# Split weights written at a start that moves by 16 bytes from one block of output columns to the next

## The chip, the cores and the metric

One Trainium2 chip; the program runs on one core. The metric is the device time of one execution, in microseconds (us). Of the kernel before there are three timed runs and one profiled execution.

## What is computed

Two decoder layers over 256 tokens of width 2048, in float32, and a last RMSNorm. Layer 0 mixes tokens by attention (compressed blocks, selected blocks and a sliding window, 16 heads), layer 1 by a chunkwise matrix memory (mLSTM, 8 heads); after each mixer comes a feed-forward part with a three-tap convolution and a gate:

```python
for i in range(DEPTH):                      # DEPTH = 2
    xn = rms_norm(x, norm_mix[i])
    x = x + mixer_i(xn)                     # nsa_mixer, then mlstm_mixer
    x = x + conv_glu_ffn(rms_norm(x, norm_ffn[i]), ...)
return rms_norm(x, norm_final)
...
def conv_glu_ffn(xn, w_up, conv_w, conv_b, w_down):
    u = xn @ w_up                           # 2048 x 11264
    c = conv_b + three taps of u along the tokens
    return (silu(c[..., :5632]) * c[..., 5632:]) @ w_down
```

Nearly all the work is in the products with weights: 2048 x 5168 into the attention, 2048 x 2048 out of it, 2048 x 6160 into the mLSTM, 2048 x 2048 out of it, and per feed-forward part 2048 x 11264 up and 5632 x 2048 down.

## The kernel before, in words

**Three matmuls for one product.** TensorE multiplies in float32r, a shortened float32. To keep float32's accuracy each operand is split into a high half (rounded to float32r) and a low half (what is left), and each product is made of high x high, high x low and low x high, all added up in one PSUM bank. The activations stand transposed in `xh` and `xl` (16 tiles of 128 x 256), later in `gh`/`gl` (feed-forward), `oh`/`ol` (attention) and `moh`/`mol` (mLSTM).

**The weights** come through `load_split` (L179 to L192): a DMA on SyncE's queue brings a piece of at most 128 x 1024 into `raw` (4 buffers), ScalarE copies it to `whi` (L189) and VectorE subtracts to get `wlo` (L191); both have 5 buffers (`SPB`). The matmuls of a piece then read `whi` and `wlo`.

**Two forms of product.** In the columns form (`cols_piece`, L217 to L230, called four times for one block of 256 output columns) the weights are the stationary operand, 128 x 128 at a time, and `xh` or `xl` is the moving one, 256 columns: L225 is xh by whi, L227 xl by whi, L228 xh by wlo. A block has 16 x 2 x 3 = 96 such matmuls. It serves the way up in the feed-forward parts (44 blocks per layer) and the queries and keys. In the rows form (`rows_mm`, L194 to L199) the activations are stationary and the weights move, 512, 416, 412, 304 or 256 columns at a time: L197 and L199 with whi, L198 with wlo. `project_out` (L308 to L344) uses it for the outputs of the mixers and for the way down, one piece of 1024 columns per 128 rows of the weight, each cut into two moving operands of 512; `rows_times` (L201 to L212) uses it for the values, gates and output gates.

**Order.** Matmuls of weights form one stream on TensorE; other work (attention, mLSTM heads, convolution) is put between pieces by hand, through the lists `evacs` and `side`, one step per `tick`. The weights run ahead of TensorE as far as the five buffers reach.

**Places in memory.** The tiles' starts within a partition follow from the order and sizes of the pools' tiles. Unused tiles were put in to shift them: `pad_w` (L75, 192 bytes), `pad_x` (L92, 64 bytes), `pad_m` (L685) and one in `ffn` (L856). In the layout of the program before, counted modulo 256 bytes, `xh` and `xl` start at 96, every buffer of `raw`, `whi` and `wlo` at 32, and `gh`, `gl`, `oh`, `ol`, `moh` and `mol` at 32. All slices of `whi`, `wlo` and the activations that matmuls read in blocks of 128, 256 or 512 columns begin at multiples of 512 bytes behind these starts; the second slice of a piece of 304, 412 or 416 columns does not (for 412 it begins 1648 bytes on).

**Two small buffers.** `q_out` (L502 to L508) makes `qu` and the rotated `qr` of a pair of heads, 3 buffers each; units of four heads read them at L548 (scores) and L523. `Head.sums` makes two tiles `y` per mLSTM head (L802 to L805, 4 buffers), which `Head.turn` reads at L812.

Of the kernel before, what the change touches and what calls it, by code (L numbers as in the profile page):

```python
# [12 lines left out]
F32 = mybir.dt.float32  # L13
F32R = mybir.dt.float32r
# [7 lines left out]
P = 128  # L22
D = 2048
KT = D // P
S = 256
# [5 lines left out]
DV = 256  # L31
# [2 lines left out]
EPS = 1e-6  # L34
QSCALE = float(np.float32(128 ** -0.5))
CAP = 15.0
NEG = -1e30

C_ID, C_MQ, C_MT, C_CA, C_C1, C_RP = 0, 0, 128, 256, 288, 320
# [4 lines left out]
def host_consts():  # L44
    c = np.zeros((P, C_N), np.float32)
    i = np.arange(P)
    c[:, C_ID:C_ID + P] = np.eye(P, dtype=np.float32)
    c[:, P + C_MQ:P + C_MQ + P] = np.where(i[None, :] <= i[:, None], 0.0, NEG)
    c[:, P + C_MT:P + C_MT + P] = np.where(i[:, None] <= i[None, :], 0.0, NEG)
    j = np.arange(NCMP)  # L50
    for t in range(NT):
        ok = (16 * j[None, :] + 31 <= (t * P + i)[:, None]) & (j[None, :] < NCMP - 1)
        c[:, P + C_CA + t * NCMP:P + C_CA + (t + 1) * NCMP] = np.where(ok, 0.0, NEG)
        c[:, P + C_C1 + t * NCMP:P + C_C1 + (t + 1) * NCMP] = np.where(ok, 1.0, 0.0)
# [8 lines left out]
def trunk(ctx: ExitStack, tc: tile.TileContext, x, positions, nsa_w_in, nsa_gate_b, nsa_cmp_pe,  # L63
# [8 lines left out]
    const = ctx.enter_context(tc.tile_pool(name="const", bufs=1))  # L72
    main = ctx.enter_context(tc.tile_pool(name="main", bufs=1))
    wpool = ctx.enter_context(tc.tile_pool(name="wpool", bufs=1))
    wpool.tile([P, 48], F32, name="pad_w")  # L75
    small = ctx.enter_context(tc.tile_pool(name="small", bufs=2))
    psum = ctx.enter_context(tc.tile_pool(name="psum", bufs=8, space=PSUM))

# [2 lines left out]
    def nm(s):  # L81
        uid[0] += 1
        return f"{s}_{uid[0]}"

    def bank():
        return psum.tile([P, 512], F32, name=nm("bank"), tag="bank")

    def fview(t):
        return t.bitcast(F32)

    h = main.tile([P, NT, D], F32, name="h")
    main.tile([P, 16], F32, name="pad_x")  # L92
    xh = main.tile([P, KT, S], F32R, name="xh")
    xl = main.tile([P, KT, S], F32R, name="xl")

# [42 lines left out]
    def rsqrt(y, v):  # L138
        t = small.tile([P, 1], F32, name=nm("rsq"), tag="rsq")
        ve.tensor_scalar(y.bitcast(I32), v.bitcast(I32), -0.5, float(0x5f3759df), op0=ALU.mult, op1=ALU.add)  # L140
        ve.tensor_scalar(v, v, -0.5, None, op0=ALU.mult)
        for _ in range(3):
            ve.scalar_tensor_tensor(t, y, v, y, op0=ALU.mult, op1=ALU.mult)
            ve.scalar_tensor_tensor(y, t, 1.5, y, op0=ALU.add, op1=ALU.mult)

    RAWB, SPB, PTB = 4, 5, 4
# [24 lines left out]
    def queued(engine):  # L171
        return tc.issue_after(fence[engine]) if engine in fence else nullcontext()
# [3 lines left out]
    def preload(w, k0, nk, c0, n):  # L176
        ready[w.tensor.name, w.offset, k0, c0] = load_split(w, k0, nk, c0, n)

    def load_split(w, k0, nk, c0, n):  # L179
        got = ready.pop((w.tensor.name, w.offset, k0, c0), None)  # L180
        if got is not None:
            return got
        view = lambda t: t[:, :nk * n].rearrange("p (k c) -> p k c", k=nk)
        raw = wpool.tile([P, 1024], F32, name=nm("raw"), tag="raw", bufs=RAWB)
        nc.sync.dma_start(view(raw), w[k0 * P:(k0 + nk) * P, c0:c0 + n].rearrange("(k p) c -> p k c", p=P))
        hi = wpool.tile([P, 1024], F32R, name=nm("whi"), tag="whi", bufs=SPB)
        lo = wpool.tile([P, 1024], F32R, name=nm("wlo"), tag="wlo", bufs=SPB)
        with queued("act"):
            latest["act"] = act(view(hi), view(raw), AF.Copy).ins  # L189
        with queued("ve"):  # L190
            latest["ve"] = ve.tensor_sub(view(lo), view(raw), fview(view(hi))).ins  # L191
        return view(hi), view(lo)  # L192
# [8 lines left out]
    def rows_times(w, c0, n, nk):  # L201
        accs = [bank() for _ in range(NT)]
        for k0 in range(0, KT, nk):
            m = min(nk, KT - k0)
            hi, lo = load_split(w, k0, m, c0, n)
            run_hooks()
            for i in range(m):
                kt = k0 + i
                for t in range(NT):
                    rows_mm(hi, lo, i, xh, xl, kt, t, accs[t][:, :n], 0, n, kt == 0, kt == KT - 1)  # L210
            tick()
        return accs  # L212
# [133 lines left out]
    def nsa(norm, nxt):  # L346
        with tc.tile_pool(name="nsa", bufs=1) as pool, tc.tile_pool(name="nsw", bufs=2) as wk:
            w = nsa_w_in[0]
# [54 lines left out]
            def rope(dst, src):  # L403
                shp = [32, 2, S]
                sw = wk.tile(shp, F32, name=nm("sw"), tag="sw", bufs=1)
                ve.stream_shuffle(sw, src, swap)
                ve.tensor_mul(sw, sw, sin[:, None, :].to_broadcast(shp))
                ve.tensor_mul(dst, src, cos[:, None, :].to_broadcast(shp))
                ve.tensor_add(dst, dst, sw)
# [91 lines left out]

            def q_out(pair, ps):  # L502
                qu = wk.tile([P, 2, S], F32, name=nm("qu"), tag="qu", bufs=3)
                qr = wk.tile([P, 2, S], F32, name=nm("qr"), tag="qr", bufs=3)
                ve.tensor_mul(qu, ps, rq[:, None, :].to_broadcast([P, 2, S]))
                act(qr, qu, AF.Copy)
                rope(qr[:32], qu[:32])
                q[pair] = (qu, qr)  # L508
# [158 lines left out]
            for pair in range(8):  # L667
                ps = cols_times(w, pair * 256)
                if pair == 1:
                    drain()  # L670
                    side.append(lambda: None)
                    side.extend(attention())
                evacs.append(partial(q_out, pair, ps))
            project_out(nsa_w_out[0], oh, ol, HEADS, nxt, gate_kt=12)

    def mlstm(norm, nxt):
        with tc.tile_pool(name="mls", bufs=1) as pool, tc.tile_pool(name="mlw", bufs=2) as wk:
            w = mlstm_w_in[0]
# [20 lines left out]
            def og_out(c, accs):  # L699
# [7 lines left out]
                if c == 4:  # L707
                    act(gp, gp, AF.Tanh, scale=float(np.float32(1 / CAP)))
                    ve.tensor_scalar(li, gp[:, :, :MH], CAP, None, op0=ALU.mult)

            def log_gates():
                act(u, gp[:, :, MH:], AF.Exp, scale=-CAP)
                ve.tensor_scalar(w1p, u, 1.0, None, op0=ALU.add)
                ve.scalar_tensor_tensor(u, w1p, 1.0, u, op0=ALU.subtract, op1=ALU.subtract)
                ve.reciprocal(lf, w1p)
                ve.tensor_mul(u, u, lf)
                act(lf, w1p, AF.Ln)
                ve.tensor_sub(lf, u, lf)
                ve.tensor_scalar(rq, norm.rbc, QSCALE, None, op0=ALU.mult)
# [39 lines left out]
            class Head:  # L759
# [18 lines left out]
                def sums(self):  # L778
                    hh, a = self.hh, self.a
                    n0, n1 = bank(), bank()  # L780
                    mm(n0[:, :DV + 1], a[:, :P], v1[:, 0, hh, :], start=True, stop=True)
                    mm(n1[:, :DV + 1], a[:, P:256], v1[:, 0, hh, :], start=True, stop=False)
                    mm(n1[:, :DV + 1], a[:, 256:384], v1[:, 1, hh, :], start=False, stop=True)
                    s = wk.tile([P, NT], F32, name=nm("mss"), tag="mss")
                    d = wk.tile([P, NT], F32, name=nm("mdn"), tag="mdn")
                    c = wk.tile([P, NT], F32, name=nm("mc"), tag="mc")
                    for t, n in enumerate((n0, n1)):
                        junk = wk.tile([P, DV], BF16, name=nm("mj"), tag="mj", bufs=1)
                        act(junk, n[:, :DV], AF.Square, scale=1.0 / 16, accum_out=s[:, t:t + 1])
                        ve.tensor_scalar(d[:, t:t + 1], n[:, DV:DV + 1], -1.0, ecol[:, t, hh:hh + 1],  # L790
                                         op0=ALU.mult, op1=ALU.max)
                        ve.tensor_tensor(d[:, t:t + 1], d[:, t:t + 1], n[:, DV:DV + 1], op=ALU.max)
                    ve.reciprocal(d, d)
                    ve.tensor_mul(s, s, d)
                    ve.tensor_mul(s, s, d)
                    ve.tensor_scalar(s, s, EPS, None, op0=ALU.add)
                    for t in range(NT):
                        rsqrt(c[:, t:t + 1], s[:, t:t + 1])
                    ve.tensor_mul(c, c, d)
                    self.y = []  # L800
                    for t, n in enumerate((n0, n1)):
                        y = wk.tile([P, DV], F32, name=nm("y"), tag="y", bufs=4)  # L802
                        ve.scalar_tensor_tensor(y, n[:, :DV], c[:, t:t + 1], sog[:, t, hh * DV:(hh + 1) * DV],
                                                op0=ALU.mult, op1=ALU.mult)
                        self.y.append(y)  # L805
# [191 lines left out]
```

## Time and profile before

| | |
|---|---|
| three timed runs | 2221.68 us median (2221.18 to 2223.4) |
| profiled execution, its own time | 2222.36 us |
| its span, first to last instruction | 2220.6 us |
| mean granted TensorE clock | 0.999 of full speed |
| busy: TensorE matmul / weight load | 99% / 92% of the span |
| busy: VectorE / ScalarE / GpSimd | 65% / 50% / 1% |
| DMA | 403 MB, 182 GB/s on average |

A record of a matmul is longer than the time by which the next one follows it, since matmuls overlap in TensorE's pipeline; what a matmul costs a full stream is read from the starts of two records and the number of matmuls between them. PE stands for the matmuls, PEld for the loads of the stationary operand, DVE for VectorE, ACT for ScalarE.

### The profile page before, as it was taken

Reading aid. Unit: us, or ns where it says so; the run is one execution under the profiler, and the core shown is the slowest. Engines: PE = TensorE matmul, PEld = TensorE weight load, DVE = VectorE, ACT = ScalarE, POOL = GpSimd, SP = SyncE. Lnnn points to the kernel's source line nnn. Section 1 sums busy time; section 2 is a strip of 40 time slices with the busy share of each in tenths; the row PEclk is TensorE's granted clock in tenths of the full one; section 3 lists DMA queues with packets and bytes.
Section 4 is the critical chain, followed back from the end, with each engine's and each line's share of the span. In section 5 each row is a group of like instructions: output and inputs, shape, how many; then the busy total and the mean of one; then the engine's idle time right before and its main releaser. Section 6 shows DMA issues by size and latency. Waiting matters only on the chain.

```text
span 2220.6 us, 37284 instructions
## 1 busy us (share of the span) xinstructions
PE 2203.8 (99%) x15072; PEld 2042.1 (92%) x15072; DVE 1444.2 (65%) x2191; ACT 1113.4 (50%) x1565; POOL 19.1 (1%) x56
## 2 busy tenths in 40 slices
PE   9999999999999999999999999999999999999998
PEld 8899789999999899998899988899999899998987
DVE  6488757676656666665645665667666566675755
ACT  6366655554445454454654444555545454454544
POOL 2000000000000000000000000000000000000000
PEclk9999999999999999999999999999999999999999
DMA  8653355666666666666567655566666666666664
GB/s 242 204 166 106 112 162 180 189 183 190 188 191 189 191 187 186 192 187 191 165 187 200 171 171 167 169 197 191 188 191 184 193 185 189 190 187 192 184 195 133
DMA packets 298317, 403.33 MB, mean 182 GB/s; under 512 B 12904, under 2 KB 256840, under 8 KB 298016
## 3 DMA queue, kind: packets, MB, share of 16 engines
q1 hardware_dynamic: 297264, 399.03, 59.6%
q8 instruction: 118, 1.93, 0.4%
q0 software_dynamic: 688, 1.83, 0.3%
q14 instruction: 55, 0.45, 0.1%
q10 hardware_dynamic: 192, 0.08, 0.0%
HBM read 398.80 MB, written 2.10 MB: 181 GB/s over the span
## 4 chain that ended last, share of the span: by engine, by line
PE 97%; DMA 1%; ACT 1%; DVE 1%; issue 0%; SPq 0%; ACTq 0%
PE bank L225 18%; PE bank L228 18%; PE bank L227 18%; PE bank L197 13%; PE bank L199 13%; PE bank L198 13%; DMA raw<-in_nsa_w_in_dram 1%; PE bank L548 1%; PE bank L259 1%; PE bank L579 0%; DMA h<-in_x_dram 0%; ACT whi L189 0%; ACT pr L552 0%; PE bank L523 0%; DVE wlo L191 0%; PE bank L597 0%
## 5 line engine op out<-in xcount | busy, mean ns | idle before, releaser
L191 DVE TENSOR_TENSOR wlo<-raw,whi 128x1024 fp32r<-128x1024 f32 (+3 forms) x755 | 912.6, 1210 | 609.8 <-ACT whi L189 607.4
L189 ACT ACTIVATE whi<-raw 128x1024 fp32r<-128x1024 f32 (+3 forms) x755 | 790.4, 1048 | 955.3 <-PE bank L227 483.5
L225 PE MATMUL bank<-xh,whi 128*128 128x256 f32 x3456 | 970.4, 281 | 3.2 <-ACT whi L189 2.6
L228 PE MATMUL bank<-xh,wlo 128*128 128x256 f32 x3456 | 965.8, 280 | 1.5 <-DVE wlo L191 1.5
L227 PE MATMUL bank<-xl,whi 128*128 128x256 f32 x3456 | 965.4, 279 | 0.1
L225 PEld LDWEIGHTS bank<-xh,whi 128*128 128x128 f32 x3456 | 649.1, 188 | 7.7 <-ACT whi L189 3.4
L228 PEld LDWEIGHTS bank<-xh,wlo 128*128 128x128 f32 x3456 | 650.1, 188 | 1.9 <-DVE wlo L191 1.9
L227 PEld LDWEIGHTS bank<-xl,whi 128*128 128x128 f32 x3456 | 648.2, 188 | 1.3 <-DVE xl L265 0.4
L197 PE MATMUL bank<-whi,gh 128*128 128x512 f32 (+1 forms) x712 | 276.1, 388 | 0.0
L199 PE MATMUL bank<-whi,gl 128*128 128x512 f32 (+1 forms) x712 | 275.5, 387 | 0.0
L198 PE MATMUL bank<-wlo,gh 128*128 128x512 f32 (+1 forms) x712 | 275.3, 387 | 0.0
L199 PEld LDWEIGHTS bank<-whi,gl 128*128 128x128 f32 x712 | 133.7, 188 | 27.4
L198 PEld LDWEIGHTS bank<-wlo,gh 128*128 128x128 f32 x712 | 133.8, 188 | 26.8
L197 PEld LDWEIGHTS bank<-whi,gh 128*128 128x128 f32 x712 | 133.7, 188 | 26.5
L197 PE MATMUL bank<-whi,xh 128*128 128x412 f32 (+4 forms) x352 | 128.0, 364 | 0.0
L199 PE MATMUL bank<-whi,xl 128*128 128x412 f32 (+4 forms) x352 | 125.2, 356 | 0.0
L198 PE MATMUL bank<-wlo,xh 128*128 128x412 f32 (+4 forms) x352 | 125.1, 355 | 0.0
L866 ACT ACTIVATE ac<-u,tapc 128x256 f32<-128x256 f32 x176 | 95.0, 587 | 3.8 <-DVE u L862 3.8
L310 DVE TENSOR_TENSOR h<-bank,h 128x512 f32<-128x512 f32 (+1 forms) x113 | 72.9, 682 | 34.5 <-PE bank L199 34.3
L862 DVE TENSOR_TENSOR u<-bank,rbc 128x512 f32<-128x512 f32 x88 | 60.8, 691 | 52.8 <-PE bank L228 52.8
L868 DVE SCALAR_TENSOR_TENSOR ac<-u,tapc,ac 128x255 f32<-128x255 f32 x176 | 77.3, 479 | 3.0 <-ACT ac L866 3.0
L870 DVE SCALAR_TENSOR_TENSOR ac<-u,tapc,ac 128x254 f32<-128x254 f32 x176 | 77.2, 479 | 0.3
(251 smaller groups left out, 1505.6 us busy)
## 6 DMA issues: line engine op xcount, KB each, us to landing
raw<-in_ffn_w_up_dram SPq DMA_DIRECT2D x352, 512.0 KB, 3.7
raw<-in_ffn_w_down_dram SPq DMA_DIRECT2D x176, 512.0 KB, 4.4
raw<-in_mlstm_w_in_dram SPq DMA_DIRECT2D x64, 512.0 KB, 3.8
raw<-in_nsa_w_in_dram SPq DMA_DIRECT2D x51, 512.0 KB, 4.6
raw<-in_nsa_w_out_dram SPq DMA_DIRECT2D x32, 512.0 KB, 3.7
raw<-in_mlstm_w_out_dram SPq DMA_DIRECT2D x32, 512.0 KB, 4.4
raw<-in_mlstm_w_in_dram SPq DMA_DIRECT2D x32, 412.0 KB, 4.1
raw<-in_nsa_cmp_w_dram SPq DMA_DIRECT2D x16, 256.0 KB, 3.4
```

Source lines behind the costliest of these rows:

```text
L189: latest["act"] = act(view(hi), view(raw), AF.Copy).ins
L191: latest["ve"] = ve.tensor_sub(view(lo), view(raw), fview(view(hi))).ins
L197: mm(o, a, hi[:, i, c:e], start=first, stop=False)
L198: mm(o, a, lo[:, i, c:e], start=False, stop=False)
L199: mm(o, b, hi[:, i, c:e], start=False, stop=last)
L225: mm(ps[:, j, :], a, xh[:, kt, :], start=(kt == 0 and j == 0), stop=False, skip_group_check=True)
L227: mm(ps[:, j, :], a, xl[:, kt, :], start=False, stop=False, skip_group_check=True)
L228: mm(ps[:, j, :], b, xh[:, kt, :], start=False, stop=(kt == KT - 1 and j == 1), skip_group_check=True)
L310: ve.tensor_add(h[:, t, a:b], acc[:, :b - a], h[:, t, a:b])
L866: act(ac[:, j, :], uu[:, j, :], AF.Identity, bias=taps[:, 3, f:f + 1], scale=taps[:, 2, f:f + 1])
L868: ve.scalar_tensor_tensor(ac[:, j, 1:], uu[:, j, :S - 1], taps[:, 1, f:f + 1], ac[:, j, 1:], op0=ALU.mult, op1=ALU.add)
L870: ve.scalar_tensor_tensor(ac[:, j, 2:], uu[:, j, :S - 2], taps[:, 0, f:f + 1], ac[:, j, 2:], op0=ALU.mult, op1=ALU.add)
```

## The change

The two padding tiles ahead of `h`'s neighbours and of the weights are gone, so `xh` and `xl` start at 32 modulo 256 bytes as all the others do. The buffers of `whi` and `wlo` grow from 1024 to 1088 elements, 4352 bytes, which is 17 x 256; their starts stay at 32 modulo 256, and so do those of all tiles behind them. Each piece is written, and read, from a place inside its buffer: `first` steps of 16 bytes for the high half, `first + apart` steps (modulo 16) for the low half. Pieces of one block of output columns share a number g; `first` is g modulo 16, and `apart` goes up by 2 after each 16 blocks. Blocks of the rows form with more than 304 columns, or with one row tile per piece, are counted apart from all others. To make room, `qr` goes from 3 buffers to 2 and `y` from 4 to 3.

```diff
+SHIFT = 64
...
-    wpool.tile([P, 48], F32, name="pad_w")
...
-    main.tile([P, 16], F32, name="pad_x")
...
+    groups_seen = {}
+
+    def offsets(w, k0, nk, c0, n):
+        rows_form = nk == 1 or n > 304
+        key = (w.tensor.name, w.offset, c0)
+        seen = groups_seen.setdefault(rows_form, {})
+        g = seen.setdefault(key, len(seen))
+        if rows_form:
+            first, apart = g % 16, 2 * (g // 16 % 4)
+        else:
+            first, apart = g % 16, 2 * (g // 16 % 8)
+        return 4 * first, 4 * ((first + apart) % 16)
...
-        hi = wpool.tile([P, 1024], F32R, name=nm("whi"), tag="whi", bufs=SPB)
-        lo = wpool.tile([P, 1024], F32R, name=nm("wlo"), tag="wlo", bufs=SPB)
+        a, b = offsets(w, k0, nk, c0, n)
+        hi = wpool.tile([P, 1024 + SHIFT], F32R, name=nm("whi"), tag="whi", bufs=SPB)[:, a:a + 1024]
+        lo = wpool.tile([P, 1024 + SHIFT], F32R, name=nm("wlo"), tag="wlo", bufs=SPB)[:, b:b + 1024]
...
-                qr = wk.tile([P, 2, S], F32, name=nm("qr"), tag="qr", bufs=3)
+                qr = wk.tile([P, 2, S], F32, name=nm("qr"), tag="qr", bufs=2)
...
-                        y = wk.tile([P, DV], F32, name=nm("y"), tag="y", bufs=4)
+                        y = wk.tile([P, DV], F32, name=nm("y"), tag="y", bufs=3)
```

## Rows read from the trace of the kernel before

**Rows 1.** The page: busy time, granted clock, chain that ended last by engine.

```profile
PE 2203.8 (99%) x15072; PEld 2042.1 (92%) x15072; DVE 1444.2 (65%) x2191; ACT 1113.4 (50%) x1565; POOL 19.1 (1%) x56
...
PEclk9999999999999999999999999999999999999999
...
PE 97%; DMA 1%; ACT 1%; DVE 1%; issue 0%; SPq 0%; ACTq 0%
```

**Rows 2.** Waits of PE's matmuls: engine, line, for whom; us in total, times, longest.

```profile
PE bank L225 <- ACT whi L189: 2.6, 2, 1.8
PE bank L228 <- DVE wlo L191: 1.5, 2, 0.8
```

**Rows 3.** Waits of ACT at the split, all of the span.

```profile
ACT whi L189 <- PE bank L227: 483.5, 358, 2.1
```

**Rows 4.** Busy by stretch (us, x): PE, PEld, DVE, ACT, POOL; clock, DMA share, GB/s.

```profile
640.14:730.48 90.34, 90.34 (x768) 90.33 (x767) 60.43 (x76) 45.25 (x53) 0.00 (x0) 1.00 0.62 187
596.59:639.91 43.32, 43.32 (x193) 35.87 (x192) 25.77 (x28) 18.60 (x19) 0.00 (x0) 1.00 0.64 191
```

**Rows 5.** Timeline of PE (start us, us, engine): way down, then eight blocks of way up.

```profile
596.60 0.40 PE L197 MATMUL bank<-whi,gh 128*128 128x512 f32 x1
...
640.15 0.28 PE L225 MATMUL bank<-xh,whi 128*128 128x256 f32 x1
...
730.61 0.40 PE L197 MATMUL bank<-whi,gh 128*128 128x512 f32 x1
```

**Rows 6.** Timeline of PE: 384 matmuls of 412 columns, then half a value block.

```profile
1108.20 0.37 PE L197 MATMUL bank<-whi,xh 128*128 128x412 f32 x1
...
1180.13 0.39 PE L197 MATMUL bank<-whi,xh 128*128 128x512 f32 x1
...
1191.09 0.40 PE L199 MATMUL bank<-whi,xl 128*128 128x512 f32 x1
```

**Rows 7.** Timeline of PE: first and last of 60 matmuls of 416 columns.

```profile
1091.69 0.44 PE L197 MATMUL bank<-whi,xh 128*128 128x416 f32 x1
...
1103.02 0.35 PE L199 MATMUL bank<-whi,xl 128*128 128x416 f32 x1
```

**Rows 8.** Timeline of PE: first and last of 30 matmuls of 256 columns, layer 1's end.

```profile
2207.97 0.28 PE L197 MATMUL bank<-whi,gh 128*128 128x256 f32 x1
...
2211.44 0.28 PE L199 MATMUL bank<-whi,gl 128*128 128x256 f32 x1
```

**Rows 9.** Timeline of PE: two stretches of 19 and 22 matmuls, attention's values.

```profile
43.96 0.28 PE L199 MATMUL bank<-whi,xl 128*128 128x256 f32 x1
...
46.00 0.28 PE L199 MATMUL bank<-whi,xl 128*128 128x256 f32 x1
...
46.91 0.28 PE L199 MATMUL bank<-whi,xl 128*128 128x256 f32 x1
...
49.39 0.28 PE L199 MATMUL bank<-whi,xl 128*128 128x256 f32 x1
```

**Rows 10.** Matmuls by shape: names, shape, count; busy, mean ns; idle before.

```profile
L225 PE MATMUL bank<-xh,whi 128*128 128x256 f32 x3456 | 970.4, 281 | 3.2 <-ACT whi L189 2.6 <-ACT xh L264 0.6
...
L197 PE MATMUL bank<-whi,gh 128*128 128x512 f32 x696 | 271.6, 390 | 0.0
...
L197 PE MATMUL bank<-whi,moh 128*128 128x512 f32 x128 | 51.2, 400 | 0.0
L197 PE MATMUL bank<-whi,oh 128*128 128x512 f32 x128 | 51.0, 399 | 0.0
```

**Rows 11.** The page's groups: the subtraction that makes wlo.

```profile
L191 DVE TENSOR_TENSOR wlo<-raw,whi 128x1024 fp32r<-128x1024 f32 (+3 forms) x755 | 912.6, 1210 | 609.8 <-ACT whi L189 607.4
```

**Rows 12.** Timeline of ACT: the third pair's copy to qr.

```profile
141.43 0.62 ACT L506 ACTIVATE qr<-qu 128x512 f32<-128x512 f32 x1
```

**Rows 13.** Chain in order of time (start us, us): scores that read the first pair.

```profile
144.87 0.86 PE bank L548 x2
145.84 0.86 PE bank L548 x2
```

**Rows 14.** Timeline of PE: first scores that read the third pair.

```profile
164.09 0.59 PE L548 MATMUL bank<-kr,qr 128*128 128x256 f32 x2
```

## The prediction

> **What bounds the kernel now.** I began with the page. Matmuls cover 99% of the span, the granted clock is at its full level in every slice (2.4 GHz, mean 0.999), and the chain that ended last is 97% TensorE [rows 1]. So there is no stage to hunt for: the time is the sum of TensorE's matmuls. Next I asked what TensorE waits for. Its two waits on split weights come to 4.1 us [rows 2]; ScalarE meanwhile waits 483.5 us for the columns form to give a weight buffer back [rows 3]. Weights are ready early, and in eight blocks of the way up VectorE is busy 60.43 us of 90.34, ScalarE 45.25 [rows 4].
>
> What is left is the time from one matmul's start to the next, the pitch. A record's own length is not it, since records overlap; I take it from starts and counts. As a yardstick I set one column per cycle at 2.4 GHz: 106.7 ns for 256 columns, 213.3 ns for 512; every pitch below lies above it. Measured:
> - columns form, whose 768 matmuls fill 640.15 to 730.61: 90.46 / 768 = **117.8 ns** [rows 5];
> - rows form with gh, 192 matmuls in 43.55 us: **226.8 ns** [rows 5];
> - rows form with xh, same shape of 512 columns, 47 steps in 10.96 us: **233.2 ns** [rows 6];
> - 412 columns, 384 in 71.93 us: 187.3 ns, 1.091 times its streaming time [rows 6]; 416 columns, 59 steps in 11.33 us: 192.0 ns, 1.108 times, pauses for other work included [rows 7];
> - 256 columns in the rows form: with gh 29 steps in 3.47 us, 119.7 ns [rows 8]; with xh 18 steps in 2.04 us, 113.3 ns, and a microsecond later 21 steps in 2.48 us, 118.1 ns [rows 9].
>
> So 6 to 12% is added to streaming, and it differs between matmuls of one shape at one clock. What differs in the program is where the two operands start. Taking the moving start minus the stationary start, modulo 256 bytes, the columns form is at +64, the rows form with gh, oh and moh at 0, that with xh at -64. At 512 columns distance 0 is the cheaper one (226.8 against 233.2); at 256 it is the dearer one (119.7 against 117.8). But place is not all: one distance ran at 113.3 and at 118.1 ns [rows 9].
>
> **The change part by part.** With xh moved to 32, columns blocks stand at distance -16 x first, rows blocks at +16 x first against gh: each block gets one of 16 distances, the low half another. No matmul, copy or DMA is added or taken away. I count blocks from the code: 110 in the first class, about seven per distance, and 38 in the second.
>
> Rows form with gh, oh, moh. These are 3 x (696 + 128 + 128) = 2856 matmuls of 512 columns [rows 10], all at the cheap distance 0. Of their 28 blocks only one gets first = 0 (96 matmuls), so 2760 leave it. The new distances are not in the trace. Bounds: below, a matmul with no more added than the 113.3 row (6.6 ns) takes 219.9, that is -6.9 ns; above, the 416 row's factor gives 236.3, +9.5 ns. I take the rows nearest in size at other distances: the value row, +6.4 (same shape), and the 412 row, whose factor gives 232.7, +5.9; its second slice stands at +48, so it speaks for more than one distance. Mean +6.1 ns x 2760 = **+16.8 us** (-19 to +26).
>
> Columns form. 3 x 3456 = 10368 matmuls [rows 10], of which one in 16 keeps its +64. Bounds: 113.3 for all, -4.5 ns, -47 us; 119.7 for all, +1.9 ns, +20 us. I take **0**: +64 in this form and -64 in the rows form agree at 118, between the two ends, and the low end was seen for 2 us only.
>
> The 384 values and some 480 matmuls of 412 and 416 columns: they are at a dear distance already and spread too. At most 6.4 ns x 864 = 5.5 us either way; I take 0.
>
> Split. L189 and L191 read and write the same amounts. Should a start off a multiple of 32 bytes slow them, the cover is VectorE's idle time, (90.34 - 60.43) / 32 pieces = 0.93 us per piece in the way up [rows 4]. L191 is the one to watch, at 1.21 us per piece [rows 11]; it would have to grow by three quarters to bind. Taken 0.
>
> `qr` with 2 buffers. The third pair's copy now runs at 141.43 us [rows 12], but the first pair is read until 145.84 + 0.86 = 146.70 [rows 13]; with two buffers the copy waits 5.3 us. The rotation on VectorE behind it waits too, and so would splits queued behind either. Up to four split pieces cover it, each 24 x 117.8 ns = 2.8 us of matmuls; the reader of the third pair comes at 164.09 [rows 14], 17 us after the buffer is free. The same falls to the fifth and seventh pair. Taken 0; without that cover 3 x 5.3 = 16 us, which would put the sum below near 2254.
>
> `y` with 3 buffers: a head's two tiles are read by its `turn`, which stands ahead of the next head's `sums` in the list of steps, so three are enough. 0.
>
> Sum: 2222.36 (profiled execution; its span is 1.8 less) + 16.8 = 2239.2. That execution is 0.7 above the median of the runs, 2221.68, so the forecast is **2238.5 us**.
>
> **The rivals.** (1) Faster: the columns form leaves the 118 state. Only starts that differ by multiples of 64 were seen at 256 columns; at others the two reads may fall into step as in the 113.3 stretch. For it: that stretch exists, and 10368 matmuls make a large lever. Against: the columns form held 117.8 through 768 matmuls, and the 412 row with its +48 is no better than the rest. It decides once the columns mean is under 117.8 - 16.8 / 10.368 = 116.2 ns; with two blocks in three at 113.3 it is -31 + 16.8, 2207.5 us, and with all but the distances 0 and +-64, 2200.
>
> (2) Slower still: most distances cost 256 columns what distance 0 does, 119.7. Then +1.9 x 10368 x 15/16 = 18.5 us more, 2257 us. For it: distance 0 itself comes up seven times. Against: 118 at two distances.
>
> (3) No change: the place of an operand does nothing, and 226.8 and 233.2 differ for another reason, such as which stage the matmuls stand in. Then 2221.7. Against: way down and values have the same shape, clock and free buffers. [...]
>
> **How the numbers follow.** A measurement of this kernel can tell a change of about 0.2%, 4.4 us, from none. Forecast 0.50, rival (1) 0.24, (2) 0.14, (3) 0.12. Faster is (1), 0.24; same is (3), 0.12; slower is the rest, 0.64. The slower cases by themselves span 2228 (rows at +6, a third of their term) to 2264 (rows at their end of +26 with columns at +16). The range over all reaches down to 2203, most of rival (1), and leaves some 0.08 on either side.
>
> **What would show it.** In the changed profile the clock and the waits of TensorE stay as they are; the count of records per line is unchanged. Right: the pitch of gh blocks differs from block to block, repeats for equal starts, and has a mean near 233; the columns blocks scatter around 118. Rival (1) shows as columns blocks at 113 to 115, rival (2) as a mean near 119.7, rival (3) as 117.8 and 226.8 in every block. Wrong in another way would be new waits of L225 or L197 on L189 or L191 between 140 and 240 us, which would put the `qr` buffer in place of the pitches.

## The result and the profile after

The changed kernel takes 2238.45 us (median of 3 runs, 2238.34 to 2239.91) against 2221.68: ratio 1.0076, interval 1.0053 to 1.0099. It is slower by 16.8 us, which is what was forecast (2238.5).

The page of the changed kernel (busy time, granted clock, chain by engine), against [rows 1]:

```profile
PE 2220.4 (99%) x15072; PEld 2045.6 (91%) x15072; DVE 1443.3 (65%) x2191; ACT 1114.4 (50%) x1565; POOL 19.0 (1%) x56
...
PEclk9999999999999999999999999999999999999999
...
PE 96%; DMA 1%; ACT 1%; DVE 1%; issue 0%; SPq 0%; ACTq 0%
```

The same number of matmuls (15072) at the same granted clock (0.999 in both), busy 16.6 us longer. Its waits, against [rows 2] and [rows 3] (L238, L240 and L241 are the former L225, L227 and L228; L202 and L204 the split; L210 to L212 the former L197 to L199):

```profile
PE bank L241 <- DVE wlo L204: 1.5, 2, 0.8
PE bank L238 <- ACT whi L202: 1.4, 2, 0.8
```

and ScalarE's wait for the columns form to give a buffer back:

```profile
ACT whi L202 <- PE bank L240: 500.6, 368, 2.2
```

TensorE waits no more than before, and ScalarE waits 17 us longer for the columns form. So the time went into the pitch. Here are the starts at which layer 0's feed-forward part turns from the way up (256 columns) to the way down (512 columns) and back. First the kernel before (timeline of TensorE: start us, us, engine; the starts between are in [rows 5]):

```profile
484.35 0.39 PE L197 MATMUL bank<-whi,gh 128*128 128x512 f32 x1
...
506.14 0.28 PE L225 MATMUL bank<-xh,whi 128*128 128x256 f32 x1
...
774.16 0.28 PE L225 MATMUL bank<-xh,whi 128*128 128x256 f32 x1
...
864.62 0.40 PE L197 MATMUL bank<-whi,gh 128*128 128x512 f32 x1
...
908.18 0.28 PE L225 MATMUL bank<-xh,whi 128*128 128x256 f32 x1
...
998.63 0.40 PE L197 MATMUL bank<-whi,gh 128*128 128x512 f32 x1
```

and the changed kernel:

```profile
486.06 0.39 PE L210 MATMUL bank<-whi,gh 128*128 128x512 f32 x1
...
508.44 0.28 PE L238 MATMUL bank<-xh,whi 128*128 128x256 f32 x1
...
598.81 0.39 PE L210 MATMUL bank<-whi,gh 128*128 128x512 f32 x1
...
643.40 0.28 PE L238 MATMUL bank<-xh,whi 128*128 128x256 f32 x1
...
734.07 0.39 PE L210 MATMUL bank<-whi,gh 128*128 128x512 f32 x1
...
778.65 0.28 PE L238 MATMUL bank<-xh,whi 128*128 128x256 f32 x1
...
869.20 0.40 PE L210 MATMUL bank<-whi,gh 128*128 128x512 f32 x1
...
914.08 0.28 PE L238 MATMUL bank<-xh,whi 128*128 128x256 f32 x1
...
1005.24 0.40 PE L210 MATMUL bank<-whi,gh 128*128 128x512 f32 x1
```

The stretch grew from 514.28 to 519.18 us, by 4.90:

| part | matmuls | before, us | after, us |
|---|---|---|---|
| way down, 512 columns | 96, 192, 192, 192 | 21.79, 43.55, 43.55, 43.56 | 22.38, 44.59, 44.58, 44.88 |
| way up, 256 columns | 4 x 768 | 90.46, 90.46, 90.46, 90.45 | 90.37, 90.67, 90.55, 91.16 |

The way down gained 3.98 us over 672 matmuls; the same starts in layer 1 give 3.48 over 672, so the mean is 5.6 ns a matmul. The way up gained 0.92 us over 3072 here and 0.99 in layer 1: 0.3 ns a matmul.

### The profile page after: what moved, and what is told of

It is laid out like the page before. It is cut to its first block, busy times and chain, and to the rows that moved or that the text cites. A ratio compares the mean times of both kernels' runs of the same rounds, so it can differ in the third digit from the quotient of the medians.

```text
span 2236.7 us, 37286 instructions
## 1 busy us (share of the span) xinstructions
PE 2220.4 (99%) x15072; PEld 2045.6 (91%) x15072; DVE 1443.3 (65%) x2191; ACT 1114.4 (50%) x1565; POOL 19.0 (1%) x56
## 4 chain that ended last, share of the span: by engine, by line
PE 96%; ACT 1%; DVE 1%; DMA 1%; issue 0%; SPq 0%; ACTq 0%
PE bank L238 18%; PE bank L240 18%; PE bank L241 18%; PE bank L210 13%; PE bank L211 13%; PE bank L212 13%; PE bank L561 1%; PE bank L272 1%; ACT pr L565 1%; DMA raw<-in_nsa_w_in_dram 0%; ACT whi L202 0%; DVE wlo L204 0%; PE bank L592 0%; PE bank L536 0%; PE bank L610 0%
## 5 line engine op out<-in xcount | busy, mean ns | idle before, releaser
L204 DVE TENSOR_TENSOR wlo<-raw,whi 128x1024 fp32r<-128x1024 f32 (+3 forms) x755 | 912.3, 1210 | 628.5 <-ACT whi L202 625.9
L202 ACT ACTIVATE whi<-raw 128x1024 fp32r<-128x1024 f32 (+3 forms) x755 | 791.1, 1049 | 972.7 <-PE bank L240 500.6
L238 PE MATMUL bank<-xh,whi 128*128 128x256 f32 x3456 | 973.7, 282 | 2.1 <-ACT whi L202 1.4
L241 PE MATMUL bank<-xh,wlo 128*128 128x256 f32 x3456 | 969.9, 281 | 1.5 <-DVE wlo L204 1.5
L240 PE MATMUL bank<-xl,whi 128*128 128x256 f32 x3456 | 970.6, 281 | 0.1
L238 PEld LDWEIGHTS bank<-xh,whi 128*128 128x128 f32 x3456 | 651.3, 188 | 6.7 <-ACT whi L202 2.3
L241 PEld LDWEIGHTS bank<-xh,wlo 128*128 128x128 f32 x3456 | 651.2, 188 | 1.9 <-DVE wlo L204 1.9
L240 PEld LDWEIGHTS bank<-xl,whi 128*128 128x128 f32 x3456 | 651.0, 188 | 1.3 <-DVE xl L278 0.4
L210 PE MATMUL bank<-whi,gh 128*128 128x512 f32 (+1 forms) x712 | 280.0, 393 | 0.0
L212 PE MATMUL bank<-whi,gl 128*128 128x512 f32 (+1 forms) x712 | 278.9, 392 | 0.0
L212 PEld LDWEIGHTS bank<-whi,gl 128*128 128x128 f32 x712 | 133.8, 188 | 31.5
L210 PEld LDWEIGHTS bank<-whi,gh 128*128 128x128 f32 x712 | 133.8, 188 | 30.1
L210 PE MATMUL bank<-whi,xh 128*128 128x412 f32 (+4 forms) x352 | 128.3, 364 | 0.0
L212 PE MATMUL bank<-whi,xl 128*128 128x412 f32 (+4 forms) x352 | 124.7, 354 | 0.0
```

The costliest lines, as they stand in the source:

```text
L210: mm(o, a, hi[:, i, c:e], start=first, stop=False)
L212: mm(o, b, hi[:, i, c:e], start=False, stop=last)
L238: mm(ps[:, j, :], a, xh[:, kt, :], start=(kt == 0 and j == 0), stop=False, skip_group_check=True)
L240: mm(ps[:, j, :], a, xl[:, kt, :], start=False, stop=False, skip_group_check=True)
L241: mm(ps[:, j, :], b, xh[:, kt, :], start=False, stop=(kt == KT - 1 and j == 1), skip_group_check=True)
```

## The experiments

All kernels below carry the change (longer buffers, no padding tiles, smaller `qr` and `y`) unless said otherwise, and differ in the two lines that choose the places. A distance is the moving start minus the stationary start, modulo 256 bytes: columns form -16 x first, rows form +16 x first against gh, oh, moh and the values' xh, which all start at 32. Where an edit is given in words, a pair such as `12, 0` stands for `first, apart`.

**Rows form back to no shift.**

```diff
         if rows_form:
-            first, apart = g % 16, 2 * (g // 16 % 4)
+            first, apart = 0, 0
```

> Of the changed kernel the rows form alone is put back to no shift (first = 0, apart = 0); the columns form keeps its moving places, the padding tiles stay away, qr has 2 buffers and y 3. Theory of the distance (the rows form pays for leaving a common start of moving and stationary operand): gh blocks back at 226.8 ns a matmul instead of 232.6, oh and moh at 227 to 228, the values (now at distance 0 as well) at 227 instead of 232; the columns mean stays at 118.5. Time 2238.5 - 16 = 2222, between 2219 and 2226. Rival (the longer buffers of 4352 bytes, the smaller qr and y, or the moved xh cost the time): it stays at 2238.

Measured: 2224.26 us, ratio 1.0013 (1.0003 to 1.0022). The start of 192 matmuls of the way down, and of what follows them:

```profile
600.29 0.39 PE L210 MATMUL bank<-whi,gh 128*128 128x512 f32 x1
...
643.84 0.28 PE L238 MATMUL bank<-xh,whi 128*128 128x256 f32 x1
```

They are at 43.55 / 192 = 226.8 ns again, and 14.2 of the 16.8 us are back. The moving places of the rows form made nearly all of the loss. The 2.7 us left over the kernel before that ran beside it (2221.59) are near what the columns form costs in the changed kernel (3.7 us, worked out further below) less 1.9 us that the values save at distance 0.

**Columns form back to one distance.**

```diff
         else:
-            first, apart = g % 16, 2 * (g // 16 % 8)
+            first, apart = 12, 0
```

> Of the changed kernel the columns form alone is put to one place for all blocks, 12 steps of 16 bytes for both halves, which gives it the distance of +64 that it had before; the rows form keeps its moving places. Theory of the distance: columns mean back to 117.8 to 118.1 ns from 118.5, 4 us less, and gh blocks still at 232.6: 2234, between 2231 and 2237. Rival (columns blocks carry the loss): 2224 or less. Rival (places in memory as such, not the distance): columns stay at 118.5 and the time at 2238.

Measured: 2227.51 us, ratio 1.0027 (1.0017 to 1.0038): 3.5 us under the lower end of what I expected. The down blocks stayed slow, as expected (44.88 us for the 192 between the two stretches shown). But the way up, at one distance and one place, ran at two pitches (starts of stretches, TensorE's timeline):

```profile
777.51 0.28 PE L238 MATMUL bank<-xh,whi 128*128 128x256 f32 x1
...
867.96 0.39 PE L210 MATMUL bank<-whi,gh 128*128 128x512 f32 x1
...
912.84 0.28 PE L238 MATMUL bank<-xh,whi 128*128 128x256 f32 x1
...
999.88 0.40 PE L210 MATMUL bank<-whi,gh 128*128 128x512 f32 x1
```

The first stretch is 90.45 / 768 = 117.8 ns a matmul, the second 87.04 / 768 = **113.3 ns**, through eight blocks without a change. Its distances, and its places modulo 256 bytes, are those of the first; what differs is the down blocks ahead of it, which stood at other places. So in this run the stream of matmuls had two steady states at one pair of distances, 117.8 and 113.3 ns. Two of the ten long stretches of the way up ran in the short one, 2 x 768 x 4.45 ns = 6.8 us less, which is why the time fell under the expected range. That the way a stretch is entered picks the state is borne out by the run of the low half further below: it has the same places and the same order of buffers in the columns form and other places in the rows form alone, and there the stretch that took 87.04 us here takes 90.45. [rows 9] had shown two pitches at one distance, 113.3 and 118.1 ns for 2 us each, in the rows form of 256 columns.

**No shift anywhere.**

```diff
         if rows_form:
-            first, apart = g % 16, 2 * (g // 16 % 4)
+            first, apart = 0, 0
         else:
-            first, apart = g % 16, 2 * (g // 16 % 8)
+            first, apart = 0, 0
```

> No shift in either form: all operands of both forms start at 32 modulo 256, distance 0 everywhere; longer buffers, no padding tiles. Theory of the distance: rows form at 226.8. For the columns form two readings stand against each other: as the 256-column rows at distance 0 before the change, 119.7 ns, which is 20 us over before, 2240; or as the changed kernel's blocks at distance 0 with the low half elsewhere, 117.7, which gives 2220. The first is what the padding tile beside xh would have been worth.

Measured: 2242.27 us, ratio 1.0092 (1.0077 to 1.0107). The first reading holds. Down blocks, then a stretch of the way up:

```profile
602.16 0.40 PE L210 MATMUL bank<-whi,gh 128*128 128x512 f32 x1
...
645.71 0.28 PE L238 MATMUL bank<-xh,whi 128*128 128x256 f32 x1
...
737.86 0.40 PE L210 MATMUL bank<-whi,gh 128*128 128x512 f32 x1
```

226.8 ns for the rows form and 92.15 / 768 = 120.0 for the columns form. Taking the padding away without moving the weights costs more than the change did: 20.7 us over the 2221.59 of the kernel before beside it. That is 2.2 ns x 10368 = 23 us in the columns form by these pitches, less some 2 us that the values save at distance 0.

**The two smaller buffers alone, in the kernel before.**

```diff
-                qr = wk.tile([P, 2, S], F32, name=nm("qr"), tag="qr", bufs=3)
+                qr = wk.tile([P, 2, S], F32, name=nm("qr"), tag="qr", bufs=2)
...
-                        y = wk.tile([P, DV], F32, name=nm("y"), tag="y", bufs=4)
+                        y = wk.tile([P, DV], F32, name=nm("y"), tag="y", bufs=3)
```

> The kernel before with the two smaller buffers alone: qr 2 instead of 3, y 3 instead of 4. Prediction's term: 0, so 2221.7, and no wait of TensorE on a split between 140 and 240 us. Rival (the third pair's copy holds ScalarE's queue and TensorE runs dry): up to 16 us more, 2238, which would be the whole loss.

Measured: 2222.73 us, ratio 1.0005 (0.9995 to 1.0014): no change that this can tell. The third pair's copy in this run (timeline of ScalarE), against [rows 12]:

```profile
147.54 0.63 ACT L506 ACTIVATE qr<-qu 128x512 f32<-128x512 f32 x1 [0.89 <-PE bank L548]
```

It runs 6.1 us later, behind the scores that read the first pair, and kept ScalarE's queue waiting for 0.89 us only, since two more splits now stand ahead of it in the queue. TensorE's only waits between 140 and 245 us are three on `pl`, 1.1 us together (0.2 before); none is on a split.

**Distance or place?** Weights of the rows form 64 bytes up, and gh and gl with them; oh and moh stay.

```diff
         if rows_form:
-            first, apart = g % 16, 2 * (g // 16 % 4)
+            first, apart = 4, 0
         else:
-            first, apart = g % 16, 2 * (g // 16 % 8)
+            first, apart = 12, 0
...
-            pool.tile([P, 48], F32, name=f"pad_f{layer}")
+            pool.tile([P, 64], F32, name=f"pad_f{layer}")
```

> Distance or place? All rows-form weights are written 64 bytes up (first = 4, apart = 0), and in the feed-forward parts gh and gl are moved up by 64 bytes too, so there the distance is 0 again at another place; oh and moh are not moved, so their distance is 64. Columns form at the distance of before (+64, both halves). Theory of the distance: gh at 226.8 to 227 ns, oh and moh at 231 to 234. Rival (the place of the weights in their buffers counts, whatever the activations' place): gh at 232 to 233 as well.

Measured: 2220.03 us in one run, beside 2220.71 of the kernel before. The down blocks and the next stretch up:

```profile
595.18 0.39 PE L210 MATMUL bank<-whi,gh 128*128 128x512 f32 x1
...
638.74 0.28 PE L238 MATMUL bank<-xh,whi 128*128 128x256 f32 x1
...
729.19 0.39 PE L210 MATMUL bank<-whi,gh 128*128 128x512 f32 x1
```

43.56 / 192 = 226.9 ns at the new place, as at the old one (226.8, [rows 5]); oh and moh, left 64 bytes off, rose from 227.6 to 229.5 ns (126 matmuls of each in one stretch). For these down blocks the distance counted, not the place. The price of +64 was 2 ns a matmul here, less than expected, where 231 to 234 ns stood for oh and moh.

**The low half alone.** Rows form `first, apart = 0, 2`, columns form `12, 0`.

> What does the low half alone do? Rows form: high half at distance 0, low half 32 bytes on (first = 0, apart = 2); columns as before the change (+64). If each matmul pays by its own distance, two in three stay at 226.8 and the third goes to 232 to 233: gh mean 228.6 to 229. If the cheap pitch needs all three at distance 0, the mean is 232 or more, as in the changed kernel's one block with first = 0 and apart = 4 (232.0).

Measured: 2235.59 us in one run.

```profile
598.13 0.40 PE L210 MATMUL bank<-whi,gh 128*128 128x512 f32 x1
...
642.92 0.28 PE L238 MATMUL bank<-xh,whi 128*128 128x256 f32 x1
...
913.42 0.28 PE L238 MATMUL bank<-xh,whi 128*128 128x256 f32 x1
...
1003.87 0.40 PE L210 MATMUL bank<-whi,gh 128*128 128x512 f32 x1
```

44.79 / 192 = 233.3 ns, though two matmuls in three stand at distance 0. From each start to the next, the matmuls of gh by whi, gh by wlo and gl by whi take 232.1, 235.8 and 232.0 ns in these 192; in the kernel before they take 227.4, 226.8 and 226.4. So in this run a matmul did not pay for its own distance alone: the 226.8 ns belonged to the whole sequence, and 32 bytes on one product of three lost all of it (233.3, against 232.2 to 233.7 in the blocks of 192 of the changed kernel shown above). The last two lines are the stretch up spoken of above, 90.45 us.

**A pair of distances for the columns form.** In the changed kernel each pair of places occurs in one block. Of the 89 blocks of the columns form that ran without a pause, the shortest was that with the high half at -64 and the low half at +64; the others took 115.6 to 121.1 ns, 72 of them 117 to 119. This block and its mirror image (high half at +64, low half at -64), each by its first start and the start behind its last matmul, in the changed kernel:

```profile
1506.52 0.28 PE L238 MATMUL bank<-xh,whi 128*128 128x256 f32 x1
...
1517.41 0.28 PE L238 MATMUL bank<-xh,whi 128*128 128x256 f32 x1
...
1597.04 0.28 PE L238 MATMUL bank<-xh,whi 128*128 128x256 f32 x1
...
1608.45 0.28 PE L238 MATMUL bank<-xh,whi 128*128 128x256 f32 x1
```

10.89 / 96 = 113.4 ns and 11.41 / 96 = 118.9 ns. The first pair is tried for all blocks, with the rows form at 0.

```diff
         if rows_form:
-            first, apart = g % 16, 2 * (g // 16 % 4)
+            first, apart = 0, 0
         else:
-            first, apart = g % 16, 2 * (g // 16 % 8)
+            first, apart = 4, 8
```

> Columns form with the high half at distance -64 and the low half at +64 for all blocks (first = 4, apart = 8), rows form at distance 0. In the changed kernel the one block with these distances ran at 113.4 ns, the shortest of all. If the pair of distances sets the pitch: all blocks at 113.3, 10368 x 4.45 ns = 46 us less than before: 2176, between 2172 and 2182. If the 113.3 state depends only on how a stretch of blocks is entered (at one pair of distances the run with the columns put back had four stretches at 113.3 and the others at 117.8): a mixture, 2190 to 2222.

Measured: **2177.22 us**, ratio 0.9803 (0.9786 to 0.9819): 43 us under the kernel before and 61 under the changed one. A stretch up between two starts of down blocks:

```profile
628.63 0.28 PE L238 MATMUL bank<-xh,whi 128*128 128x256 f32 x1
...
715.69 0.40 PE L210 MATMUL bank<-whi,gh 128*128 128x512 f32 x1
...
759.24 0.28 PE L238 MATMUL bank<-xh,whi 128*128 128x256 f32 x1
```

87.06 / 768 = 113.4 ns and 43.55 / 192 = 226.8 ns. All ten long stretches of the way up run so. With this pair the state did not depend on how a stretch is entered, here and in two later runs with other places in the rows form (87.06 and 87.04 us for 768).

**The mirror image**, in both forms: columns `12, 8`, rows `4, 8`.

> The mirror image of the pair, in both forms: columns with the high half at +64 and the low half at -64 (first = 12, apart = 8), rows form with the high half at +64 and the low half at -64 against gh, oh and moh (first = 4, apart = 8). If what counts is that the halves stand 128 bytes apart, columns at 113.3 here too. If the order of the signs counts, columns at 117.8 as in the changed kernel's neighbours. Rows form: unknown pair; every other place measured for gh gave 229 to 235, so 232 by that; 220 if the pair does for 512 columns what it does for 256.

Measured: 2228.52 us in one run; rows form 230.4 ns, and the columns form again in two states:

```profile
366.88 0.36 PE L238 MATMUL bank<-xh,whi 128*128 128x256 f32 x1
...
481.22 0.39 PE L210 MATMUL bank<-whi,gh 128*128 128x512 f32 x1
...
503.34 0.28 PE L238 MATMUL bank<-xh,whi 128*128 128x256 f32 x1
...
594.64 0.40 PE L210 MATMUL bank<-whi,gh 128*128 128x512 f32 x1
```

114.34 / 1008 = 113.4 ns in the first stretch of the layer, 91.30 / 768 = 118.9 in the next. So halves 128 bytes apart were not enough to hold the short state; the signs counted, with 118.9 ns here where the pair run has 113.4. This run changed the rows form as well, and so the way in, but the one block of the mirrored pair in the changed kernel, entered from another block of the columns form, took 118.9 ns too. Neither the 113.3 nor the 117.8 of the expectation was met by the long stretches at 118.9.

**Can the rows form do better?** Twice with the columns form of the pair run: rows `12, 8` (the pair itself), then rows `0, 8`.

> Columns form as in the pair run (high half at -64, low half at +64), and now the rows form at the same pair against gh, oh and moh (first = 12, apart = 8). If the pair does for 512 columns what it does for 256, gh goes under 226.8, to 220 at best (the same 6.6 ns over streaming), 2856 matmuls x 6.8 ns = 19 us under the pair run, 2158. If distance 0 for all three is the best state of the rows form: gh at 230 to 233, as at every other place so far, 2188 to 2195.

> Columns form as in the pair run; rows form with the high half at distance 0 and the low half 128 bytes on (first = 0, apart = 8). With the low half 32 or 64 bytes on, gh ran at 233.3 and 232.0. If any difference between the halves breaks the cheap state: gh at 230 to 234, 2188 to 2197. If halves 128 bytes apart are what helped the columns form: gh at 226.8 or less, 2177 or less.

Measured: 2188.94 and 2189.17 us, one run each; in the first the down blocks take

```profile
586.34 0.39 PE L210 MATMUL bank<-whi,gh 128*128 128x512 f32 x1
...
630.72 0.28 PE L238 MATMUL bank<-xh,whi 128*128 128x256 f32 x1
...
717.78 0.39 PE L210 MATMUL bank<-whi,gh 128*128 128x512 f32 x1
```

44.38 / 192 = 231.1 ns, and in the second 44.37, the same. Of the places tried in the rows form none went under the 226.8 ns of distance 0 for all three. Both runs also enter the way up from other places than the pair run did, and the stretch stays at 87.06 and 87.04 us.

**Both halves at -64 in the columns form**, rows at 0.

> Which part of the pair is it? Columns form with both halves at -64 (first = 4, apart = 0), rows form at distance 0. If the high half at -64 is enough: 113.3 in all stretches, 2177. If the two halves must differ: 117.8 or a mixture by the way a stretch is entered, as with both halves at +64, 2200 to 2223.

Measured: 2216.98 us in one run, a mixture. The long stretches are at 117.8 ns; a stretch of 144 among the mLSTM's keys and queries is at the short pitch:

```profile
504.60 0.28 PE L238 MATMUL bank<-xh,whi 128*128 128x256 f32 x1
...
595.05 0.40 PE L210 MATMUL bank<-whi,gh 128*128 128x512 f32 x1
...
1257.01 0.37 PE L238 MATMUL bank<-xh,whi 128*128 128x256 f32 x1
...
1273.43 0.40 PE L210 MATMUL bank<-whi,xh 128*128 128x512 f32 x1
```

90.45 / 768 = 117.8 and 16.42 / 144 = 114.0. Of the pairs run in all blocks, only -64 with +64 held the short state (113.4 ns).

## Why the prediction was right

- **Rows form, +16.8 us: right in kind, a little high.** The pitch was taken as +6.1 ns; gh measured +5.6. 126 matmuls with moh went from 28.67 us to 29.26, +4.7 ns, and 126 with oh rose by 6.3, but those between pauses rose less (84 of moh by 2.0 ns). Summed from each matmul's start to the next start, gh gained 11.6 us, oh 1.8 and moh 0.9: the term measured 14.3 us. The reason given, that the common start of gh and the weights is a cheap state (226.8 ns) and the others resemble the value row, is shown by three runs: put back, the loss goes; moved together, the pitch stays at 226.9; one half moved, the cheap state is gone.
- **Counting each matmul by itself** (2760 leave, 96 stay) was wrong as a picture: with the low half alone moved, all three paid (232.1, 235.8 and 232.0 ns). Here it cost nothing, because the one block with first = 0 also had its low half elsewhere; it ran at 232.0 ns.
- **Columns form, 0: nearly.** It is +0.3 ns in the long stretches and 3.7 us over all 10368, inside the bounds of -4.5 and +1.9 ns. But the ground given, that +64 and -64 agree at 118 and so 118 is what most distances cost, missed that both ends of the bound are steady states of this stream: 113.3 was seen for 2 us before the change and set aside for that. It is the longer lever of this kernel: in the pair run the columns form takes 44 us less than before.
- **The yardstick** of 106.7 and 213.3 ns (one column per cycle, with the clock in GHz) was my assumption: the pages give the clock only as a share of full speed. What the runs show is what 256 columns more cost at distance 0: 226.8 - 120.0 = 106.8 ns in the run with no shift. The lower bound of 219.9 ns, which carries the 6.6 ns of the 113.3 row over to 512 columns, was met by no run; the lowest there is 226.8.
- **Values and 412 columns, 0: nearly.** The values went from 233.2 to 231.3 ns in the stretch of 48, 0.6 us over all 384; with the other matmuls of the rows form outside gh, oh and moh it is 0.8 us less.
- **Split, `qr`, `y`, 0: right.** The buffers alone measured 1.0005; L204 has the mean of L191, 1210 ns, and L202 takes 1049 where L189 took 1048, with about half of the starts at odd multiples of 16 bytes.
- **The sum** is 14.3 + 3.7 - 0.8 = 17.2 us; all other matmuls (start-up, attention, heads) and the pauses by them take 1.1 us less, which makes the 16.1 us of the span. That the forecast of 2238.5 met the measured 2238.45 us to a tenth is luck: the rows form was put 2.5 us too high and the columns form 3.7 us too low, and the values, the other work and the pauses took the difference back.
- **The sign "repeats for equal starts"** can't be read as it was meant, since no pair of places comes twice. The high half's place alone does not set the pitch: with the high half at -64 six blocks took 113.4 to 118.9 ns by the place of the low half.
- **Rival (1)** fell for the mean of all distances (117.8 + 0.3 = 118.1 ns against the 116.2 at which it would have decided), and holds for one pair. **Rival (2)** fell by the same mean; 120.0 is what distance 0 in all halves does. **Rival (3)**, by which the place changes nothing, falls by the first three runs and the pair run. In these runs 256 columns took 113.3 to 120.0 ns in the long stretches of the columns form as the places alone changed, and gh's 512 columns took 226.8 to 235.5.

Not settled: what in the chip makes the states. That two reads fall into step, as rival (1) has it, was a guess; no run separates the reads of the moving operand from the load of the next stationary one. That the entry of a stretch picks its state was seen (117.8 or 113.3 ns at the same places), and how it does so was not explained.

## What to carry to other kernels

Where TensorE is busy throughout, take the pitch from starts and counts, block by block, and compare it with what more columns cost at the same clock; here that was 106.8 ns for 256, and the pitches of 113.3 to 120.0 ns, and of 226.8 for 512 columns, hid 6 to 12% over it under a busy share of 99%. Then try the start of the moving against that of the stationary operand in steps of 16 bytes, each product form by itself and all operands of a repeating sequence together. A sweep over blocks within one run, as this change is, cost 0.8% here and shows what to fix: here it named the pair that made the kernel 2% faster than it was before. A block's pitch in such a sweep may depend on the block ahead of it, since one pair of distances had two states (117.8 and 113.3 ns), so a pair has to be run in all blocks before it is trusted.

## What the runs showed of the hardware that was not expected

In these runs a stream of float32r matmuls of 256 columns, each with its own stationary operand, ran at several steady pitches at the same granted clock (0.998 to 0.999 of full speed): 117.8 ns in the kernel before, 113.3 with the columns form put back, 118.9 in the mirror image and 120.0 with no shift. At the same places modulo 256 bytes two of them occurred, 117.8 and 113.3 with the columns form put back, 118.9 and 113.4 in the mirror image, and a state once entered lasted through its stretch of 768 or 1008 matmuls. 512 columns with gh took 226.8 ns with all three matmuls of the sequence at distance 0 (the kernel before, and the run with no shift), 233.3 with one of them 32 bytes off (the low half alone), and 228.9 to 235.5 in the blocks of the changed kernel.
